# A streaming-encoder block: VectorE's sums of weight blocks in one sequence, gate multiplications later, a gate block's joins and second heads sooner, other first loads

## The chip, the cores and the metric

One core of one Trainium2 chip runs the whole program. The metric is the device time of one execution in microseconds, as the median of the timed runs.

## The reference

The input x has 256 tokens of width 2048, in float32, as all weights have. One layer is computed; every matrix product is in float32 accuracy.

```python
x = x + 0.5 * swiglu(rms_norm(x, ffn1_norm), w_gate, w_up, w_down)      # hidden width 5632
h = rms_norm(x, mix_norm)
u, q, k, v, g, a_lr = split(h @ w_in)      # pool part | linear attention with 4 heads, gate g
x = x + concat([pool_mixer(u), gla_mixer(q, k, v, g, a_lr)]) @ w_out
x = x + mem_cross_attention(rms_norm(x, xattn_norm), rms_norm(mem, mem_norm), w_q, w_kv, w_o)
x = x + 0.5 * swiglu(rms_norm(x, ffn2_norm), w_gate2, w_up2, w_down2)
out = rms_norm(x, final_norm)

def swiglu(h, w_gate, w_up, w_down):
    return (silu(h @ w_gate) * (h @ w_up)) @ w_down
```

In the mixer, the linear attention's output of each head is normalised (a factor per token and head), scaled, and multiplied by silu(g).

## The kernel before

**Units.** All weights are read once, in units of 1 MB (a tile of 128 x 2048 float32 called `raw`). A unit is loaded by SyncE into one of three `raw` tiles, split, and multiplied. The split makes two tiles of it: ScalarE casts the block to fp32r (`wh`, line 239) and VectorE subtracts that from the block (`wl`, line 240, "the low part"). A product in float32 accuracy is then three matmuls, activations-high by `wh`, activations-high by `wl`, activations-low by `wh`. `wh` and `wl` have three buffers each, so a unit can be split while the two before it are multiplied. The activations stand in `xs` (and `ys`) as a high and a low half, made by ScalarE and VectorE (lines 216 and 217).

**The stream.** `Stream` holds the list of units and of other operations (`st.op(f, after)`: `f` is traced once `after` more units have been listed). `emit` traces unit u's matmuls after the splits of units up to u + 2 (u + 1 for the first four), and a unit's load after the split of the unit three before it. Before the split of unit n, `prepare` of unit n + 1 is traced.

**Order on an engine.** The tracing order gives priorities; a scheduler then orders the instructions of each engine by its own estimate of when their inputs are there, so that what is traced later may be issued sooner. Some orders are forced: `in_turn(engine, f)` queues `f`'s instruction behind the last one so recorded on that engine (`latest`), and `behind_weights(f)` queues what `f` traces behind the last recorded ones of VectorE and ScalarE. The splits of the weights are traced with `in_turn`. A tile pool gives its buffers out again once they have been read; the tile `j` (a work space) has one buffer, and serves the squares for the row norms (line 255) and the sums of activations (`Sums.make`, lines 370 to 382).

**The feed-forward blocks.** The hidden width is cut into parts of 4, 4 and 3 blocks of 512 columns. For pairs of blocks, a gate product, an up product (eight units each) and then a down product are made. In most of them some units (0, 2 and 4 of `range(8)` for gate and up) are multiplied with seven products instead of eight (`seven`, line 435), which needs sums of weight blocks (tile `T`, made by `add_weights` on VectorE in three adds, lines 397, 400 and 401; then cast and split as weights are) and sums of activations (tile `xe`, made by `Sums.make`). `T` has one buffer. `combine` and `join` (lines 491 to 505) put the partial results together. The gate result goes through Silu on ScalarE with a row factor `Rcol` (line 741); `late_up` (line 749) multiplies gate by up; it is done for the first pair of a part while the next pair's gate product runs, and `turn` (line 759) transposes the result for the down product. The first gate product is a plain one (`block_t`, line 318).

**The opening.** SyncE loads alternately weights and columns of x (`wwide`, `load_x`). TensorE transposes x (`x_chunk`, line 632), ScalarE and VectorE make `xs` of it. The squares of x give the row norms (`x_squares`, `finish_norm`, lines 261 and 192 to 204), which the first gate eviction needs as `Rcol`.

**The gate blocks of the mixer.** `block_a` (line 303) multiplies four units and then evicts two halves with `evict(p, ps)`, here `ev_g(b)`: `joined` copies one half of a PSUM tile on ScalarE (line 276) and adds the other on VectorE (line 277). Between them lie the heads of the linear attention: `scores` (line 1022), `attend` (lines 1035 and 1038), `head_norms` (line 1057), `head_scale` (spread at line 213, applied at line 1071), two heads for each b. PSUM has four tiles (`ps`), which all of these share.

Of the kernel before, what the change touches and what calls it, by code (L numbers as in the profile page):

```python
# [92 lines left out]
def build(ctx, tc, I, out):  # L93
# [177 lines left out]
        R = rows["R"] = scope["pool"].tile([P, S], F32, tag="R", name=uid("R"))  # L271
        nc.vector.tensor_copy(R, ps[:, 0, :S])

    def joined(ps, dst, scale=None):
        c = ctile()
        nc.scalar.copy(c, ps[:, :, S:])
        nc.vector.tensor_tensor(out=dst, in0=ps[:, :, :S], in1=c, op=ALU.add)  # L277
        if scale is not None:
            nc.vector.tensor_tensor(out=dst, in0=dst, in1=bc(scale), op=ALU.mult)

# [112 lines left out]
    def add_weights(u, raw):  # L393
        t = scope["pool"].tile([P, 4 * NB], F32, tag="T", name=f"T{u}")
        w = raw.rearrange("p (b n) -> p b n", n=NB)
        v = t.rearrange("p (b n) -> p b n", n=NB)
        nc.vector.tensor_tensor(  # L397
            out=v[:, 0:2], in0=w[:, 1:3], in1=w[:, 0:1].to_broadcast([P, 2, NB]), op=ALU.add
        )
        nc.vector.tensor_tensor(out=v[:, 2], in0=v[:, 0], in1=w[:, 2], op=ALU.add)  # L400
        nc.vector.tensor_tensor(out=v[:, 3], in0=v[:, 2], in1=w[:, 3], op=ALU.add)  # L401
        return t

    def split_seven(u, raw, t):
# [149 lines left out]
    def wwide(w, n0, k0=0, nk=KT):  # L554

        def src(k):
            def load(raw):
                raw = raw.rearrange("p (k n) -> p k n", n=2 * NB)
                if len(loaded) < 3:
                    for kk in range(2):  # L560
                        parts = (0, NB) if not loaded else (0,)
                        for c in parts:
                            n = 2 * NB // len(parts)
                            wload(raw[:, kk : kk + 1, c : c + n], w, k + kk, 1, n0 + c, n)
                            next(first_loads, None)
                else:
                    wload(raw, w, k, 2, n0, 2 * NB)
                loaded.append(1)
            return load
        return [src(k0 + k) for k in range(0, nk, 2)]  # L570
# [154 lines left out]
    def ffn(wg, wu, wd, down):  # L725
# [36 lines left out]
            split(ys[:, k : k + 4, 0, :], ys[:, k : k + 4, 1, :], v)  # L762

        for i, g in enumerate(PAIRS):
            st.op(lambda g=g: x_sums.make(g), 5 + i)
        for lo, n in FF_PARTS:
            whole = n == KT // 4
            for b in range(0, n - 1, 2):
                n0 = (lo + b) * NB
                if lo == b == 0:  # L770
                    block_t(wwide(wg, n0), xs, lambda j, ps: ev_gate(j, ps, 1))
                else:
                    block_s(wwide(wg, n0), xs, x_sums, range(8), lambda j, c: ev_gate(j, c, 0))
                held, up = {}, {}
                into_down = whole and b
                block_s(wwide(wu, n0), xs, x_sums, range(8), up.__setitem__)
                st.op(lambda held=held: held.update(gate))
                for j in (1, 0):
                    st.op(lambda j=j, held=held, up=up: late_up(held, j, up[j]),
                          0 if into_down else 2)  # L780
                wait = CLEAR if b + 2 < n - 1 else 1 if into_down else 4
                for j in range(2):
                    st.op(lambda j=j, b=b, held=held: turn(held[j], 4 * (b + j)), wait)
            if n % 2:
                def both(j, ps):
                    if j:
                        ev_up(0, ps)
                    else:
                        ev_gate(j, ps, 1)
                block_t(wtwo(wg, wu, (lo + n - 1) * NB), xs, both)  # L790
                st.op(lambda n=n: turn(gate[0], 4 * (n - 1)), 1)
            if whole:
                for g, after in zip(Y_PAIRS, (2, 4)):
                    st.op(lambda g=g: behind_weights(lambda: y_sums.make(g)), after)
            down(wd, 4 * lo, 4 * n, lo + n == FF // NB, y_sums if whole else None)
# [277 lines left out]
    def ev_g(b):  # L1073
        def evict(p, ps):
            h = 2 * b + p
            t = ttile()
            joined(ps, t, rows["R"])
            nc.scalar.activation(t, t, AF.Silu)
            for vt in range(2):
                nc.vector.scalar_tensor_tensor(  # L1080
                    out=t[:, vt, :], in0=mix["oz", b][:, 2 * p + vt, :], scalar=gcol(G_HN + 2 * h + vt),
                    in1=t[:, vt, :], op0=ALU.mult, op1=ALU.mult,
                )
            split_pair(ys, 8 + 2 * h, t)
        return evict

    for b in range(2):
        block_b(wblock(w_in, (4 + b) * NB), xs, ev_v(b))
        for i in range(2):
# [2 lines left out]
            st.op(lambda h=h: scores(h), at)  # L1092
            st.op(lambda h=h: attend(h), at + 1)
            st.op(lambda h=h: head_squares(h), at + 1)
        st.op(lambda b=b: head_norms(b), 4)
        st.op(lambda b=b: head_scale(b), 5)
    block_a(wblock(w_in, 6 * NB), xs, ev_g(0))
    block_a(wblock(w_in, 7 * NB), xs, ev_g(1))
    st.op(close_scope, 1)
    st.op(open_scope("s_x"), 1)  # L1100
# [275 lines left out]
    def split_unit(u, own):  # L1376
# [11 lines left out]
        step = {0: NB, 1: 2 * NB, 2: 2 * NB}.get(u, 4 * NB)  # L1388
        for c in range(0, 4 * NB, step):
            part = slice(c, c + step)  # L1390
            split_weights(hi[:, part], lo[:, part], raw[:, part])
        return (hi, lo), None

# [38 lines left out]
```

## Time and profile before

| | us |
|---|---|
| median of 3 runs | 2137.97 (2135.68 to 2138.45) |
| profiled execution | 2137.34 |
| its span, first to last instruction | 2135.5 |
| TensorE busy (matmuls) | 2110.5, 99% of the span |
| VectorE busy | 1528.0, 72% |
| ScalarE busy | 1036.1, 49% |
| mean granted TensorE clock | 0.997 |

The profile calls the engines PE (TensorE, matmuls), PEld (TensorE, weight loads), DVE (VectorE), ACT (ScalarE), POOL (GpSimd) and SP (SyncE, which issues the loads). "pt<-wh,xs" is an instruction that writes tile pt and reads wh and xs; L240 is line 240 of the kernel. "A <- B: 2.6, 1, 1.3" in the waits says that A waited for B for 2.6 us in total, how many times, and the longest. In the chain of waits a row has start, length and what ran then. PEclk is the share of full speed that TensorE's clock was granted.

### The profile page before, as it was taken

What the parts mean: (1) busy time and instruction counts of PE and PEld (TensorE: products, weight loads), DVE (VectorE), ACT (ScalarE), POOL (GpSimd) and SP (SyncE); (2) the same over time, 40 slices, a digit from 0 to 9 for tenths busy, and PEclk for the clock granted to TensorE, in tenths of its full rate; (3) what the DMA queues carried; (4) which work ended last, traced back from release to release, by engine and by line L of the source; (5) the groups of instructions that cost most, each with busy time, mean ns of one, the idle gap of its engine ahead of it and who ended that gap; (6) DMA issues with size and microseconds to landing.
All of it is one profiled execution on the core that took longest, in us unless ns stands there. A gap on an engine that the chain in (4) does not pass through costs nothing.

```text
span 2135.5 us, 24222 instructions
## 1 busy us (share of the span) xinstructions
PE 2110.5 (99%) x10008; PEld 1764.6 (83%) x10008; DVE 1528.0 (72%) x1332; ACT 1036.1 (49%) x928; POOL 14.0 (1%) x40
## 2 busy tenths in 40 slices
PE   9999999999999999999999999999999999999998
PEld 7778888788888888878888888888888887888886
DVE  7888888888865677565656545467888878888744
ACT  7544444544543545446445444455444455444434
POOL 0000000000000000000000000000000000000001
PEclk9999999999999999999999999999999999999999
DMA  7556665566666655458655455665577655676663
GB/s 277 197 177 217 238 215 192 182 218 237 215 214 220 218 180 178 158 169 297 224 178 178 158 166 170 197 210 198 183 236 230 224 180 192 219 237 217 234 217 118
DMA packets 143606, 435.93 MB, mean 204 GB/s; under 512 B 9860, under 2 KB 13544, under 8 KB 143112
## 3 DMA queue, kind: packets, MB, share of 16 engines
q1 hardware_dynamic: 143464, 434.38, 60.4%
q8 instruction: 78, 1.28, 0.2%
q14 instruction: 32, 0.26, 0.0%
q10 hardware_dynamic: 32, 0.01, 0.0%
HBM read 417.58 MB, written 16.78 MB: 203 GB/s over the span
## 4 chain that ended last, share of the span: by engine, by line
PE 94%; DVE 3%; ACT 1%; issue 1%; DMA 0%; SPq 0%; DVEq 0%; ACTq 0%
PE pt L318 53%; PE pa L303 15%; PE pt L435 13%; PE pb L318 6%; PE pe L318 3%; DVE wl L240 1%; PE ph L759 1%; ACT wh L239 1%; DVE xl L240 1%; PE pl L1166 1%; PE pv L1201 1%; PE px L688 0%; DVE T L397 0%; PE pp L886 0%; DVE sg L749 0%
## 5 line engine op out<-in xcount | busy, mean ns | idle before, releaser
L240 DVE TENSOR_TENSOR wl<-raw,wh 128x2048 fp32r<-128x2048 f32 (+2 forms) x316 | 712.3, 2256 | 399.3 <-ACT wh L239 398.8
L239 ACT CAST wh<-raw 128x2048 fp32r<-128x2048 f32 (+2 forms) x316 | 594.9, 1884 | 561.3 <-PE pt L318 338.0
L318 PE MATMUL pt<-wh,xs 128*128 128x512 f32 x1952 | 620.8, 390 | 3.0 <-ACT wh L239 1.7
L318 PE MATMUL pt<-wh,ys 128*128 128x512 f32 x1536 | 477.4, 390 | 0.0
L318 PEld LDWEIGHTS pt<-wh,xs 128*128 128x128 f32 x1952 | 366.3, 188 | 79.6 <-ACT wh L239 2.6
L318 PE MATMUL pt<-wl,xs 128*128 128x512 f32 x976 | 380.5, 390 | 0.0
L318 PEld LDWEIGHTS pt<-wh,ys 128*128 128x128 f32 x1536 | 288.0, 188 | 59.6
L303 PE MATMUL pa<-xs,wh 128*128 128x512 f32 x896 | 317.9, 399 | 3.1 <-DVE t L277 2.6
L318 PE MATMUL pt<-wl,ys 128*128 128x512 f32 x768 | 298.9, 389 | 0.0
L303 PE MATMUL pa<-xs,wl 128*128 128x256 f32 x896 | 248.9, 281 | 0.0
L239 ACT CAST wh<-T 128x2048 fp32r<-128x2048 f32 x66 | 126.2, 1912 | 246.9 <-DVE T L401 218.7
L240 DVE TENSOR_TENSOR wl<-T,wh 128x2048 fp32r<-128x2048 f32 x66 | 151.2, 2290 | 94.0 <-ACT wh L239 94.0
L318 PEld LDWEIGHTS pt<-wl,xs 128*128 128x128 f32 x976 | 183.2, 188 | 38.2 <-DVE wl L240 0.3
L303 PEld LDWEIGHTS pa<-xs,wh 128*128 128x128 f32 x896 | 168.3, 189 | 42.5 <-issue 3.3
L303 PEld LDWEIGHTS pa<-xs,wl 128*128 128x128 f32 x896 | 169.7, 190 | 1.5
L318 PEld LDWEIGHTS pt<-wl,ys 128*128 128x128 f32 x768 | 144.2, 188 | 29.6
L318 PE MATMUL pb<-wh,xs 128*128 128x512 f32 x384 | 121.5, 392 | 0.0
L240 DVE TENSOR_TENSOR xl<-raw,xh 128x1536 fp32r<-128x1536 f32 x66 | 115.5, 1750 | 1.2 <-ACT xh L239 1.2
L435 PE MATMUL pt<-wh,xe 128*128 128x512 f32 x324 | 109.9, 393 | 2.6 <-ACT wh L239 2.6
L239 ACT CAST xh<-raw 128x1536 fp32r<-128x1536 f32 x66 | 97.6, 1478 | 15.1 <-PE pt L435 7.9
L318 PEld LDWEIGHTS pb<-wh,xs 128*128 128x128 f32 x384 | 72.1, 188 | 15.0 <-issue 0.2
L435 PE MATMUL pt<-xh,xs 128*128 128x512 f32 x216 | 80.6, 390 | 3.2 <-DVE sg L505 2.1
(231 smaller groups left out, 1919.9 us busy)
## 6 DMA issues: line engine op xcount, KB each, us to landing
raw<-in_ffn_w_down SPq DMA_DIRECT2D x88, 1024.0 KB, 5.6
raw<-in_ffn_w_up SPq DMA_DIRECT2D x80, 1024.0 KB, 5.0
raw<-in_ffn_w_gate SPq DMA_DIRECT2D x77, 1024.0 KB, 5.0
raw<-in_w_in SPq DMA_DIRECT2D x32, 1024.0 KB, 5.2
raw<-in_xattn_w_kv SPq DMA_DIRECT2D x32, 1024.0 KB, 5.2
raw<-in_w_out SPq DMA_DIRECT2D x16, 1024.0 KB, 6.3
raw<-in_xattn_w_q SPq DMA_DIRECT2D x16, 1024.0 KB, 5.1
raw<-in_xattn_w_o SPq DMA_DIRECT2D x16, 1024.0 KB, 5.6
```

The costliest lines, as they stand in the source:

```text
L239: in_turn("scalar", lambda: nc.scalar.copy(hi, src))
L240: in_turn("vector", lambda: nc.vector.tensor_tensor(out=lo, in0=src, in1=f32(hi), op=ALU.subtract))
L303: nc.tensor.matmul(o, w, x, start=k == 0 and i == 0, stop=last and i == 1)
L318: nc.tensor.matmul(ps, a, w, start=first and i == 0, stop=last and i == 2)
L435: nc.tensor.matmul(banks[n], x, w, start=n in fresh and j == 0, stop=n in ends and j == 2)
L759: nc.tensor.transpose(v[:, i, h * P : (h + 1) * P], g[:, h, i * P : (i + 1) * P], ident)
L1166: nc.tensor.matmul(ps[:, t, :M], ys[:, 4 * h + d, a, tok], xa["K"][:, d, b, :], start=i == 0, stop=i == 11,)
L1201: nc.tensor.matmul(ps[:, d, :S], xa["V"][:, m, a, col], xa["PT"][:, m, b, :], start=i == 0, stop=i == 5,)
```

## The change

1. *Sums in one sequence.* The three adds of `add_weights` are traced with `in_turn("vector", ...)`. Since `prepare` of unit n + 1 is traced ahead of the split of unit n, they are queued on VectorE behind the low part of unit n - 1 and ahead of that of unit n, with no low part between them.
2. *Gate multiplications later.* `late_up` of a part's first pair, where another pair follows, is traced three units after the up product instead of two.
3. *Sums of activations.* `Sums.make` for gate and up is traced after 4, 5 and 6 units instead of 5, 6 and 7, and queued behind the weights' split. This puts the first two of them ahead of the squares in the tracing order.
4. *The gate block.* For the first gate block both evictions are traced right after its last unit (before, the second one unit later), and the adds of its joins are recorded as `latest`, so that later low parts are queued behind them. `head_norms` and `head_scale` of the first heads come one unit later, `head_norms` of the second heads one unit sooner.
5. *First loads.* The first columns of x follow two weight pieces instead of one. In the first unit, the casts after the first quarter are queued behind the high halves of the first `xs`.

```diff
-    def joined(ps, dst, scale=None):
+    def joined(ps, dst, scale=None, first=False):
         c = ctile()
         nc.scalar.copy(c, ps[:, :, S:])
-        nc.vector.tensor_tensor(out=dst, in0=ps[:, :, :S], in1=c, op=ALU.add)
+        add = nc.vector.tensor_tensor(out=dst, in0=ps[:, :, :S], in1=c, op=ALU.add)
+        if first:
+            latest["vector"] = add
...
     def add_weights(u, raw):
...
-        nc.vector.tensor_tensor(
-            out=v[:, 0:2], in0=w[:, 1:3], in1=w[:, 0:1].to_broadcast([P, 2, NB]), op=ALU.add
-        )
-        nc.vector.tensor_tensor(out=v[:, 2], in0=v[:, 0], in1=w[:, 2], op=ALU.add)
-        nc.vector.tensor_tensor(out=v[:, 3], in0=v[:, 2], in1=w[:, 3], op=ALU.add)
+        for o, a, b in (
+            (v[:, 0:2], w[:, 1:3], w[:, 0:1].to_broadcast([P, 2, NB])),
+            (v[:, 2], v[:, 0], w[:, 2]),
+            (v[:, 3], v[:, 2], w[:, 3]),
+        ):
+            in_turn("vector", lambda: nc.vector.tensor_tensor(out=o, in0=a, in1=b, op=ALU.add))
...
                             wload(raw[:, kk : kk + 1, c : c + n], w, k + kk, 1, n0 + c, n)
-                            next(first_loads, None)
+                            if c or loaded:
+                                next(first_loads, None)
+                    if len(loaded) == 2:
+                        next(first_loads, None)
...
         for i, g in enumerate(PAIRS):
-            st.op(lambda g=g: x_sums.make(g), 5 + i)
+            st.op(lambda g=g: behind_weights(lambda: x_sums.make(g)), 4 + i)
...
                     st.op(lambda j=j, held=held, up=up: late_up(held, j, up[j]),
-                          0 if into_down else 2)
+                          0 if into_down else 3 if b + 2 < n - 1 else 2)
...
-            joined(ps, t, rows["R"])
+            joined(ps, t, rows["R"], b == 0)
...
-        st.op(lambda b=b: head_norms(b), 4)
-        st.op(lambda b=b: head_scale(b), 5)
-    block_a(wblock(w_in, 6 * NB), xs, ev_g(0))
+        st.op(lambda b=b: head_norms(b), 5 - 2 * b)
+        st.op(lambda b=b: head_scale(b), 6 - b)
+    block_a(wblock(w_in, 6 * NB), xs, ev_g(0), (0, 0))
...
         for c in range(0, 4 * NB, step):
             part = slice(c, c + step)
+            if u == 0 and c == step:
+                latest["scalar"] = rows["hi", 0]
             split_weights(hi[:, part], lo[:, part], raw[:, part])
```

## The prediction

> **What bounds the kernel now.** I read the page first, then the waits of TensorE, then the chain of waits in the stretches around each wait, last the timeline of single engines there.
>
> ```profile
> span 2135.5 us, 24222 instructions
> PE 2110.5 (99%) x10008; PEld 1764.6 (83%) x10008; DVE 1528.0 (72%) x1332; ACT 1036.1 (49%) x928; POOL 14.0 (1%) x40
> ```
>
> TensorE is busy for all but 25 us of the span, and the change takes no matmul away. So it can win only idle time of TensorE, and time in which TensorE runs slowly. The profiled execution took 2137.34 us (1.8 us lie outside the span); the median of the three timed runs is 2137.97, 0.6 more. I make the sum as a difference and take it from the median. About 0.2% (4.3 us) is what a measurement of this kernel can tell from no change.
>
> The waits of TensorE (us in total, times, longest) name nearly all of the idle time that other engines cause:
>
> ```profile
> PE pa L303 <- DVE t L277: 2.6, 1, 2.6
> PE pt L435 <- ACT wh L239: 2.6, 2, 1.3
> PE pt L435 <- DVE sg L505: 2.1, 2, 1.7
> PE pt L318 <- ACT wh L239: 1.7, 2, 0.8
> ...
> PE pt L318 <- ACT xs L216: 1.4, 1, 1.4
> PE pt L435 <- ACT sg L741: 1.1, 1, 1.1
> PE pt L435 <- DVE xl L240: 0.8, 1, 0.8
> ...
> PE po L1035 <- DVE ST L1028: 0.6, 1, 0.6
> ```
>
> That is 12.9 us in some ten places, each up to 2.6 us long, where VectorE or ScalarE came late. The edits can be set against them one by one.
>
> **Sums in one sequence, gate multiplications later.** The second and fourth rows are one place that occurs twice, in FFN 1 and at the same step of FFN 2. The chain of waits there (start, us, what):
>
> ```profile
> 367.76 2.29 DVE wl L240
> 370.05 2.65 DVE sg L749 x4
> 372.70 1.13 DVE T L397
> 373.83 1.67 DVE xl L240
> ...
> 376.94 0.06 ACT wh L239
> ```
>
> VectorE does four gate multiplications (L749), then the first block sum (L397), a low part (xl) and the other two sums; only then can ScalarE cast the sums (wh), for which TensorE waits. The change takes both things out of the way: the multiplications of a first pair of hidden blocks come one unit later, behind the next sums and low parts, which takes 2.65 us off the front; and xl may no longer stand between the sums, another 1.67. The two waits in a row at one place are (2.6 + 1.7) / 2 = 2.1 us, so 4.3 us off covers it. What is late next is the landing of the raw block, or the low part that the sums now go ahead of: that is the slower rival below. The moved multiplications still stand well before the transposes that read them, six units on, and hold up plain low parts only.
>
> After this wait, and after the 2.6 us one at 914 us, TensorE also ran slowly (columns: stretch; sum of PE, PEld, DVE, ACT, POOL busy; PEclk; DMA):
>
> ```profile
> 381.00:383.00 2.00, 1.99 (x6) 1.42 (x6) 2.00 (x2) 1.44 (x1) 0.00 (x0) 0.63 0.10 41
> 383.00:385.00 2.00, 2.00 (x7) 1.55 (x6) 2.00 (x2) 0.59 (x1) 0.00 (x0) 0.52 0.35 55
> 914.00:916.00 2.00, 1.81 (x5) 1.59 (x6) 2.00 (x5) 0.00 (x0) 0.00 (x0) 0.50 0.74 152
> 916.00:918.00 2.00, 2.00 (x9) 1.73 (x8) 1.90 (x5) 1.43 (x3) 0.00 (x0) 0.65 0.88 356
> ```
>
> The granted clock falls to a half. Over 4 us the mean was (0.63 + 0.52) / 2 = 0.58 and (0.50 + 0.65) / 2 = 0.58, so each place lost 4 x 0.42 = 1.7 us more. I count this as won with the wait. [...] The trace shows the drop after idle times of 2.6 us and less, so I go by the trace.
>
> FFN 1 gives 2.1 + 1.7 and FFN 2, whose clock stayed whole, 2.1: 5.9 us at most. I take 5.0; the ends are 5.9 and nothing.
>
> A third place, in the next block, waits first for a low part (the 0.8 us row, xl) and then for a join (L505, 2.1 - 1.7 = 0.4 us) that stands behind it. The sums' sequence changes what lies there but gives the join no right of way: I take half, 0.6 us, between 1.2 and nothing. The longer join wait (1.7 us), elsewhere, I leave as it is.
>
> **The gate block.** The longest wait stands where the first gate block ends, in the chain of waits:
>
> ```profile
> 911.02 2.30 DVE wl L240
> 913.33 0.02 issue
> 913.35 0.70 DVE t L277
> ```
>
> and ScalarE's half of the join was long done:
>
> ```profile
> 907.41 0.59 ACT L276 COPY c<-pa 128x512 f32<-128x512 f32 x1 [2.59 <-PE pa L303]
> ```
>
> The join add (t L277) could have run at 908.0; it stood behind a later block's low part (wl) and came at 913.35. The next gate block needs the PSUM tile that the add reads. In the changed kernel both joins of this block are traced at its end and the next low part is queued behind their adds, so the add comes 5.3 us sooner, twice what TensorE waited. The reordered heads help too: the second heads' products no longer take their PSUM tile behind the first heads' scaling, so the 0.6 us wait (po L1035), which falls in the same gap, moves into the block before. Behind the adds waits one low part, for a unit two units away: 2 x 0.7 us, covered. I take 2.6 + 0.6 + 1.7 of clock = 4.9 us; ends 5.3 and nothing.
>
> **The start.** TensorE, then ScalarE:
>
> ```profile
> 4.39 2.00 PE L632 MATMUL px<-ident,x 128*128 128x128 f32 x8
> 7.75 0.50 PE L318 MATMUL pt<-wh,xs 128*128 128x512 f32 x1 [1.36 <-ACT xs L216]
> ```
>
> ```profile
> 6.70 0.62 ACT L239 CAST wh<-raw 128x512 fp32r<-128x512 f32 x1 [1.30 <-DMA raw<-in_ffn_w_gate]
> 7.22 0.83 ACT L216 ACTIVATE xs<-px,gains 128x256 fp32r<-128x256 f32 x2
> ```
>
> The activations (xs) stand behind the second quarter's cast, which waited for its DMA. The change queues that cast behind them and loads the weight pieces before the x columns. The 1.4 us wait should nearly go: a lead of 1.1 us.
>
> It will not last. The lead runs on to the first up block, where TensorE waits for the first gate eviction (sg L741, the 1.1 us row), and that for the row factors:
>
> ```profile
> L255 ACT ACTIVATE j<-x x16: 406/418/428, 15.3 to 46.4; 128x256 f32<-128x256 f32 x16
> L255 ACT ACTIVATION_READ_ACCUMULATOR j<-x x16: 185/190/211, 15.6 to 46.7; 128x1 f32 x16
> L370 DVE TENSOR_TENSOR j<-xs x3: 670/681/683, 10.6 to 60.8; 128x512 f32<-128x512 f32 x3
> ```
>
> ```profile
> 33.78 2.29 DVE L240 TENSOR_TENSOR wl<-raw,wh 128x2048 fp32r<-128x2048 f32 x1 [1.64 <-ACT wh L239]
> ...
> 48.82 0.16 DVE L261 TENSOR_REDUCE sums<-ss 128x2 f32<-128x16 f32 x1
> ...
> 60.74 0.15 DVE L204 RECIPROCAL Rcol<-chain 128x2 f32<-128x2 f32 x1
> ```
>
> From reduction to factor it takes 12 us, small VectorE steps with big ones between them. The squares (L255) and the activations' sums (L370) share one tile, j. Before, the first sums went ahead of the squares and the second waited for the last of them. In the changed kernel two sums are traced ahead of the squares, the second behind the low part that here ran 33.78 to 36.07. If j goes round in the order of the trace, no square can run before about 38 us (36.1, the add of 0.68, four smaller steps and the split), and 16 squares at 0.42 with a read-out of 0.19 each, which overlap a little, are some 9 us: they end at 47 to 50 instead of 47. Against that, one set of sums less lies in VectorE's way afterwards. Bounds for start and opening together: 2 us better (the lead and the 1.1 us wait for sg) to 3 worse (squares 3 us later). I take nothing.
>
> **New small waits.** Each of the 66 sums now goes ahead of the low part of the unit before it. One sequence costs (timeline of VectorE)
>
> ```profile
> 484.41 1.22 DVE L397 TENSOR_TENSOR T<-raw 128x1024 f32<-128x1024 f32 x1
> 485.66 0.69 DVE L400 TENSOR_TENSOR T<-T,raw 128x512 f32<-128x512 f32 x1
> 486.39 0.69 DVE L401 TENSOR_TENSOR T<-T,raw 128x512 f32<-128x512 f32 x1
> ```
>
> 2.7 us, and at this place it already stands ahead of the next low part, and the waits above hold none of this place. I put 1.5 us for waits elsewhere, between 0 and the 13 us of the slower rival below.
>
> **Sum:** 5.0 + 0.6 + 4.9 + 0 - 1.5 = 9.0 us off 2137.97: 2129.0.
>
> **The rivals.** *Low parts come late (slower).* Place: units before a block sum in the tight gate and up blocks. VectorE and TensorE there:
>
> ```profile
> 415.80 2.29 DVE L240 TENSOR_TENSOR wl<-raw,wh 128x2048 fp32r<-128x2048 f32 x1
> ...
> 420.42 0.39 PE L318 MATMUL pt<-wl,xs 128*128 128x512 f32 x1
> ```
>
> The low part is ready at 418.09, 2.3 us before TensorE uses it; pushed back by a 2.7 us sequence it is 0.4 us late. If the sums then also wait for a raw block, the low part waits with them. It decides from the point where VectorE does not win back as much by earlier casts. If about 35 of the 66 (where the sums now follow that low part) lost 0.4 us, that is 14 us instead of my 1.5: about 2142. Against it: VectorE is busy only 72%, and in these blocks it sat idle waiting for the cast of the sums, which the new order fills.
>
> *The row factors come later.* The opening loses the 3 us by which the squares may end later, and a wait that long may drop the clock for 1.7 us as at 914 us: 2132 to 2133.7. For it stands the shared tile; against it, that fewer steps lie between reduction and factor.
>
> *The waits only move.* A scheduler orders each engine's queue, and the added edges change its whole order; TensorE's queue too is interleaved from several units. Waits may come back at other places, as large: about 2138.
>
> **How the numbers follow.** Forecast 0.62 (its own range 2123 to 2134), late low parts 0.16, late row factors 0.10, waits that move 0.12. Faster by over 0.2% (below 2133.7): 0.60 from the forecast, 0.07 from late row factors, 0.01 from moved waits: 0.68. Within 0.2%: 0.02 + 0.03 + 0.09 = 0.14. Slower: 0.16 + 0.02 = 0.18. The range 2123 to 2140 takes in the best end of the start, the late row factors, the moved waits and the mild part of the late low parts.
>
> **What would show it.** In the profile after, the waits of TensorE should have no row for t L277 and none for wh L239 under L435 beyond 1 us; PEclk should be whole around 380 and 910 us; L749 should come behind a wl from T; L397, L400 and L401 should follow each other 66 times with 0.04 us between; the first L318 matmul should start near 6.5 us. If a row "PE pt <- DVE wl L240" of several us with many times appears, the slower rival is right; if "PE pt L435 <- ACT sg L741" grows, the row factors are late. I am wrong if the waits sum to 12 us or more again.

## The result, and the profile after

The changed kernel takes 2131.97 us (2129.47 to 2133.83, 7 runs) where the kernel before takes 2138.23 (2135.43 to 2140.49): a ratio of 0.9971, with a 95% interval of 0.996 to 0.9983. That is 6.3 us faster; 9.0 were forecast. The profiled execution of the changed kernel took 2133.83 us, its slowest, so that the two traces differ by 3.5 us of span only.

The page of the changed kernel, its span and the busy time of each engine:

```profile
span 2132.0 us, 24229 instructions
PE 2109.4 (99%) x10008; PEld 1766.1 (83%) x10008; DVE 1530.9 (72%) x1332; ACT 1043.3 (49%) x928; POOL 12.9 (1%) x40
```

The work is the same. The waits of TensorE, of which this is all that the view has (us in total, times, longest; the lines have moved by 3 to 7, so that L439 is L435 of before, L321 is L318, L748 is L741):

```profile
PE pt L439 <- ACT sg L748: 6.9, 1, 6.9
PE px L639 <- DMA x<-in_x: 2.8, 1, 2.8
PE pwarm L186 <- POOL ident masks.py:199: 1.4, 1, 1.4
PE pt L439 <- DVE wl L240: 1.4, 1, 1.4
PE pa L306 <- DVE xs L217: 0.4, 1, 0.4
```

Every wait that the prediction quoted from the middle of the kernel is gone: the block sums' casts, the low part xl, both joins, the gate block's add. Two new ones of 6.9 and 2.8 us stand in the first 75 us. So the change won in the body and paid at the opening.

**The body.** Groups of instructions (busy, mean ns | idle of the engine before them, and what ended it). Before:

```profile
L239 ACT CAST wh<-T 128x2048 fp32r<-128x2048 f32 x66 | 126.2, 1912 | 246.9 <-DVE T L401 218.7 <-PE pt L318 21.3 <-issue 6.6
L240 DVE TENSOR_TENSOR wl<-T,wh 128x2048 fp32r<-128x2048 f32 x66 | 151.2, 2290 | 94.0 <-ACT wh L239 94.0
```

After:

```profile
L239 ACT CAST wh<-T 128x2048 fp32r<-128x2048 f32 x66 | 126.4, 1915 | 116.5 <-PE pt L321 75.5 <-DVE T L405 27.0 <-issue 13.6
L240 DVE TENSOR_TENSOR wl<-T,wh 128x2048 fp32r<-128x2048 f32 x66 | 151.0, 2287 | 22.7 <-ACT wh L239 22.7
L405 DVE TENSOR_TENSOR T<-raw 128x1024 f32<-128x1024 f32 x66 | 80.7, 1223 | 23.7 <-DMA raw<-in_ffn_w_gate 12.4 <-DMA raw<-in_ffn_w_up 10.1 <-DMA raw<-in_ffn_w_down 0.6
```

ScalarE waited 218.7 us for finished block sums, now 27.0; VectorE in turn waited 94.0 us for the cast of the sums, now 22.7. The sums themselves now wait 23.7 us for landing blocks, and none of that reaches TensorE. At the place in FFN 1 where the first of the forecast waits stood, VectorE's timeline after reads:

```profile
370.56 2.28 DVE L240 TENSOR_TENSOR wl<-T,wh 128x2048 fp32r<-128x2048 f32 x1
372.88 1.23 DVE L405 TENSOR_TENSOR T<-raw 128x1024 f32<-128x1024 f32 x1
374.14 1.42 DVE L405 TENSOR_TENSOR T<-T,raw 128x512 f32<-128x512 f32 x2
...
382.01 2.73 DVE L756 SCALAR_TENSOR_TENSOR sg<-sg,Rcol,sg 128x512 f32<-128x512 f32 x4
```

The three adds run one behind the other, and the multiplications (L756, before L749) come behind the next low part from T. Both stretches with a slow clock are whole (stretch; sum of PE, PEld, DVE, ACT, POOL busy; PEclk; DMA share; GB/s). The third row is the new slow one:

```profile
69.00:76.00 7.00, 3.79 (x10) 3.00 (x11) 0.86 (x2) 5.11 (x7) 0.00 (x0) 0.52 0.00 0
377.00:381.00 4.00, 4.00 (x19) 3.31 (x18) 3.62 (x3) 2.34 (x2) 0.00 (x0) 1.00 0.52 152
905.00:915.00 10.00, 10.00 (x61) 8.90 (x61) 5.35 (x8) 2.93 (x3) 0.00 (x0) 1.00 0.50 143
```

**Where the 3.5 us come together.** The start of one and the same matmul in both traces, first down product, first logits, last down product. Before:

```profile
185.28 0.39 PE L318 MATMUL pt<-wh,ys 128*128 128x512 f32 x1
...
1160.35 0.28 PE L1166 MATMUL pl<-K,ys 128*128 128x256 f32 x1
...
2059.58 0.39 PE L318 MATMUL pe<-wh,ys 128*128 128x512 f32 x1
```

After:

```profile
195.26 0.39 PE L321 MATMUL pt<-wh,ys 128*128 128x512 f32 x1
...
1159.92 0.28 PE L1173 MATMUL pl<-K,ys 128*128 128x256 f32 x1
...
2056.10 0.39 PE L321 MATMUL pe<-wh,ys 128*128 128x512 f32 x1
```

At 195 us the changed kernel is 10.0 us behind, although the join wait at 141 us (1.85 us between the two matmuls beyond their usual distance) has gone: the opening costs 11.8. The rest of FFN 1 gives back 6.1, the gate block 4.8, FFN 2 3.0; some 0.4 is lost again between these.

**The opening.** First the start, TensorE after:

```profile
4.38 1.11 PE L639 MATMUL px<-ident,x 128*128 128x128 f32 x4
8.32 1.12 PE L639 MATMUL px<-ident,x 128*128 128x128 f32 x4 [2.82 <-DMA x<-in_x]
9.08 0.78 PE L321 MATMUL pt<-wh,xs 128*128 128x512 f32 x1
```

The first matmul of the product starts at 9.08, not 7.75. It is not the cast or xs that it waits for: the transposes of the second columns of x stand ahead of it in TensorE's queue (as they did before, at 4.39), and those columns' load is now issued behind a second weight piece, at 2.19 instead of 1.73, and lands at 8.27 instead of 5.43. A landing this late does not come with the order each time: e1, e2 and e12 below issue the same loads in the same order, and there TensorE waits 1.3, 0.8 and 1.1 us for it instead of 2.8, while with the loads as before it waits 1.0 us or less in ten traces. Until about 14.3 us the matmuls then follow at 0.42 us, before at 0.23. Next, the squares (duration in ns min/median/max, first and last start):

```profile
L255 ACT ACTIVATE j<-x x16: 408/418/421, 56.0 to 65.8; 128x256 f32<-128x256 f32 x16
```

They ran from 15.3 to 46.4 before. They wait for tile j, which the first two sums of activations now hold, the second last; VectorE's timeline shows how long (j, and xe made from it):

```profile
42.19 0.68 DVE L373 TENSOR_TENSOR j<-xs 128x512 f32<-128x512 f32 x1
...
43.39 0.29 DVE L380 TENSOR_TENSOR j<-j 128x128 f32<-128x128 f32 x1
...
46.40 0.29 DVE L381 TENSOR_TENSOR j<-j 128x128 f32<-128x128 f32 x1
...
48.66 0.28 DVE L382 SCALAR_TENSOR_TENSOR j<-j 128x128 f32<-128x128 f32 x1
...
51.52 0.29 DVE L385 TENSOR_TENSOR j<-j 128x128 f32<-128x128 f32 x1
...
53.25 0.69 DVE L246 TENSOR_TENSOR xe<-j,xe 128x512 fp32r<-128x512 f32 x1
...
66.93 0.16 DVE L261 TENSOR_REDUCE sums<-ss 128x2 f32<-128x16 f32 x1
69.03 0.17 DVE L204 RECIPROCAL Rcol<-chain 128x2 f32<-128x2 f32 x1
```

Six steps of 2.5 us together take 11.7 us, since a low part or a block sum lies between any two of them. After two casts of ScalarE the squares start at 56.0; with another cast between them they end at 66.3, the factor comes at 69.2 instead of 60.9, and TensorE waits 6.9 us for the first gate eviction. On ScalarE the eviction comes 1.7 us behind the factor: the cast of the third sums and a table load for the eviction's line stand between. Before, both were done while the eviction waited for the factor. ScalarE, before:

```profile
57.22 1.28 ACT L741 ACT_TABLE_LOAD   x1
60.93 1.27 ACT L741 ACTIVATE sg<-pt,Rcol 128x512 f32<-128x512 f32 x2 [2.42 <-DVE Rcol L204]
```

After:

```profile
69.59 1.28 ACT L748 ACT_TABLE_LOAD   x1
70.89 1.27 ACT L748 ACTIVATE sg<-pt,Rcol 128x512 f32<-128x512 f32 x2
```

### The profile page after: what moved, and what is told of

The parts are those of the page before. It is cut to its first block, busy times and chain, and to the rows that moved or that the text cites. A ratio compares the mean times of both kernels' runs of the same rounds, so it can differ in the third digit from the quotient of the medians.

```text
span 2132.0 us, 24229 instructions
## 1 busy us (share of the span) xinstructions
PE 2109.4 (99%) x10008; PEld 1766.1 (83%) x10008; DVE 1530.9 (72%) x1332; ACT 1043.3 (49%) x928; POOL 12.9 (1%) x40
## 3 DMA queue, kind: packets, MB, share of 16 engines
q8 instruction: 78, 1.28, 0.2%
## 4 chain that ended last, share of the span: by engine, by line
PE 98%; ACT 1%; DVE 0%; DMA 0%; issue 0%; SPq 0%; DVEq 0%; ACTq 0%
PE pt L321 56%; PE pa L306 15%; PE pt L439 15%; PE pb L321 6%; PE pe L321 3%; PE ph L766 1%; PE pl L1173 1%; PE pv L1208 1%; PE px L695 0%; ACT j L255 0%; DMA x<-in_x 0%; PE pp L893 0%; ACT wh L239 0%; PE px L639 0%; PE pa L920 0%; PE po L1042 0%
## 5 line engine op out<-in xcount | busy, mean ns | idle before, releaser
L321 PE MATMUL pt<-wh,xs 128*128 128x512 f32 x1952 | 618.4, 391 | 0.0
L321 PE MATMUL pt<-wh,ys 128*128 128x512 f32 x1536 | 477.2, 390 | 0.0
L321 PEld LDWEIGHTS pt<-wh,xs 128*128 128x128 f32 x1952 | 367.3, 188 | 75.9
L321 PE MATMUL pt<-wl,xs 128*128 128x512 f32 x976 | 380.8, 390 | 0.0
L321 PEld LDWEIGHTS pt<-wh,ys 128*128 128x128 f32 x1536 | 288.0, 188 | 59.4
L321 PE MATMUL pt<-wl,ys 128*128 128x512 f32 x768 | 299.0, 389 | 0.0
L321 PEld LDWEIGHTS pt<-wl,xs 128*128 128x128 f32 x976 | 183.8, 188 | 38.2 <-DVE wl L240 0.2
L306 PEld LDWEIGHTS pa<-xs,wh 128*128 128x128 f32 x896 | 167.7, 188 | 39.7 <-DVE xs L217 0.8
L321 PEld LDWEIGHTS pt<-wl,ys 128*128 128x128 f32 x768 | 144.2, 188 | 29.8
L240 DVE TENSOR_TENSOR wl<-T,wh 128x2048 fp32r<-128x2048 f32 x66 | 151.0, 2287 | 22.7 <-ACT wh L239 22.7
L321 PE MATMUL pb<-wh,xs 128*128 128x512 f32 x384 | 121.6, 392 | 0.0
L439 PE MATMUL pt<-wh,xe 128*128 128x512 f32 x324 | 111.0, 390 | 0.0
L405 DVE TENSOR_TENSOR T<-raw 128x1024 f32<-128x1024 f32 x66 | 80.7, 1223 | 23.7 <-DMA raw<-in_ffn_w_gate 12.4
L405 DVE TENSOR_TENSOR T<-T,raw 128x512 f32<-128x512 f32 x132 | 90.9, 689 | 2.7
```

What stands on the lines that cost most here:

```text
L240: in_turn("vector", lambda: nc.vector.tensor_tensor(out=lo, in0=src, in1=f32(hi), op=ALU.subtract))
L306: nc.tensor.matmul(o, w, x, start=k == 0 and i == 0, stop=last and i == 1)
L321: nc.tensor.matmul(ps, a, w, start=first and i == 0, stop=last and i == 2)
L405: in_turn("vector", lambda: nc.vector.tensor_tensor(out=o, in0=a, in1=b, op=ALU.add))
L439: nc.tensor.matmul(banks[n], x, w, start=n in fresh and j == 0, stop=n in ends and j == 2)
```

## The experiments

Kernels with the same time in the column "before" share the runs of the kernel before; kernels of different groups are compared by their ratios. "Factor" is when the last step of the row factors ends (L204), "gate wait" the wait of TensorE for the first gate eviction (sg).

| kernel | us | before | ratio, 95% | factor at | gate wait |
|---|---|---|---|---|---|
| after | 2131.97 | 2138.23 | 0.9971 (0.996 to 0.9983) | 69.2 | 6.9 |
| e1 sums of activations as before | 2123.46 | 2139.15 | 0.9927 (0.9915 to 0.994) | 61.8 | 1.1 |
| e2 squares in a tile of their own | 2126.88 | 2139.15 | 0.9945 (0.9933 to 0.9958) | 62.2 | 3.0 |
| e3 loads as before | 2130.86 | 2139.15 | 0.9962 (0.995 to 0.9975) | 65.3 | 7.1 |
| e7 e1 and e3 together | 2120.14 | 2139.15 | 0.9911 (0.9898 to 0.9925) | 50.6 | none |
| e4 gate block alone | 2134.17 | 2138.43 | 0.998 (0.9971 to 0.9989) | 63.7 | 1.1 |
| e5 later multiplications alone | 2137.41 | 2138.43 | 0.9996 (0.9987 to 1.0005) | 61.1 | 1.1 |
| e6 sums in sequence alone | 2129.87 | 2138.43 | 0.9966 (0.9954 to 0.9979) | 62.3 | 1.1 |
| e8 e7 without the cast's place | 2124.88 | 2138.43 | 0.9941 (0.9929 to 0.9954) | 63.2 | 1.1 |
| e9 e2 and e3 together | 2120.81 | 2137.57 | 0.9918 (0.9905 to 0.9932) | 51.4 | none |
| e10 e7 with multiplications as before | 2121.74 | 2137.57 | 0.9927 (0.9915 to 0.994) | 50.5 | none |
| e11 e7 with the second columns later | 2124.32 | 2137.57 | 0.9939 (0.9925 to 0.9952) | 61.2 | 1.1 |
| e12 sums early, not queued | 2124.12 | 2137.57 | 0.9936 (0.9924 to 0.9949) | 61.6 | 1.3 |

The theory: the loss lies in the opening alone, and there in the sums of activations (part 3 of the change), which hold the squares' tile; the new loads cost a smaller part. The rivals: the loads are the main loss; or the squares come late for another reason, VectorE's or ScalarE's order.

### Which edit of the opening costs what

**e1**, from the changed kernel:

```diff
-            st.op(lambda g=g: behind_weights(lambda: x_sums.make(g)), 4 + i)
+            st.op(lambda g=g: x_sums.make(g), 5 + i)
```

> The changed kernel, with the sums of activations traced and ordered as before (after 5, 6 and 7 units, not behind the weights); all else of the change stays. Theory (the squares wait for the tile j, which the second sums now hold first): the row factors come some 8 us sooner than in the changed kernel, the 6.9 us wait of TensorE for the gate eviction shrinks to under 2.5 us, and the time falls by about 8 us, ratio to before 0.993. Rival (the block sums in one sequence push the norm's small steps back on VectorE): the wait stays within 2 us of 6.9 and the ratio stays 0.997.

0.44% less than after by the ratios, 9.4 us. The waits of TensorE in e1 have

```profile
PE pt L439 <- ACT sg L748: 1.1, 1, 1.1
```

The gate wait is what it was before the change, and the mean clock of the profiled execution is 0.999 (0.997 in after). The theory holds, and with its size. In the trace the first matmul is sooner as well, at 7.52 with the same loads, by the earlier landing named above.

**e2**, from the changed kernel: the sums of activations stay where the change put them, the squares get another tile (in bfloat16, for room; the squares are written there and not read, only their sums are).

```diff
-            j = tmp.tile([P, S], F32, tag="j", name=uid("j"))
+            j = tmp.tile([P, S], mybir.dt.bfloat16, tag="q", name=uid("q"))
```

> The changed kernel, with one edit: the squares write their (unused) products to a tile of their own, in bfloat16 so that it fits; the row sums stay float32. The sums of activations stay early and behind the weights. Theory (shared tile): squares run again from about 16 us on, the factors are there near 60 us, the ratio falls to about 0.993 as in the run with the sums as before. Rival (it is the place of the sums on VectorE, not the tile): the squares move but the wait stays above 5 us, ratio 0.997.

0.26% less than after, 5.6 us: the shared tile is most of what e1 takes back. The squares run from 9.7 to 47.1 and the reduction at 48.8, as before the change. It stays short of the expectation, although the factor comes at 62.2, nearly as in e1 (61.8). The third sums are still early and queued: their cast ends only at 62.16 on ScalarE, the table load of 1.28 us follows it, and the eviction starts at 63.47. In e1 cast and table load are done by 59.4, and the eviction starts at 61.81, with the factor. The gate wait of 3.0 us is followed by a stretch at half clock (same columns as above):

```profile
64.00:70.80 6.80, 6.01 (x14) 4.76 (x15) 1.11 (x1) 3.79 (x5) 0.00 (x0) 0.50 0.00 0
```

6.0 us of work at half speed are 3.0 us lost.

**e3**, from the changed kernel:

```diff
-                            if c or loaded:
-                                next(first_loads, None)
-                    if len(loaded) == 2:
-                        next(first_loads, None)
+                            next(first_loads, None)
```

> The changed kernel, with the first loads in the order of before (x columns and weight pieces in turn from the start); the cast's place in the first unit stays. Theory (the transposes of the second x columns stand ahead of the first matmul on TensorE, so their late landing delays it by 2.8 us and leaves the clock at a half until 14 us): the first matmul comes at 6.5 to 7 us instead of 9.1, clock whole from about 6 us, the start gains 4 us; since the row factors still come late, 2 to 4 us of that reach the end, ratio 0.9955. Rival (the opening ends at the row factors, whatever the start): ratio 0.997, the wait for the gate eviction grows by what the start gained.

The first matmul starts at 6.59 us, 2.5 sooner, and the wait for x falls to 0.3 us. When the clock became whole there, expected at about 6 us, is not shown here. By the ratios 1.9 us are left at the end (0.9962 and 0.9971), but the intervals overlap, and theory and rival cannot be told apart by them. In the trace the gate wait is about as long, 7.1 us, and not longer by what the start gained, as the rival had it; the first down product starts at 192.62, 2.6 us sooner: the factor moves with the start (65.3 instead of 69.2), and a longer drop of the clock takes back a part (mean 0.53 from 64 to 75 us, which is some 10.3 us at half; 6.8 in after).

**e7**, both edits together:

> The changed kernel with both the sums of activations and the first loads as before. Theory: the opening's whole loss goes, 11 to 12 us of the changed kernel's time by the profiles: about 2122, ratio 0.992. Rival (the two losses hide one another, so that taking both away gives no more than the larger): 2124, as with the sums alone.

This is the lowest ratio of all, 19.0 us below the kernel before, and 0.9911 against 0.9971 for the change as it was made. e1 was timed in the same rounds, and each of its times (2123.1 to 2124.0) lies above each of e7's (2118.9 to 2121.4): with the sums as before, the loads cost 3.3 us by the medians. Its waits, but for the constant 1.4 us at the very start and 0.4 for xs:

```profile
PE pt L321 <- DVE wl L240: 0.9, 1, 0.9
PE pt L439 <- DVE sg L509: 0.8, 2, 0.7
```

No gate wait is left at all; the kernel before had one of 1.1 us, so this opening is shorter than that one too (first down product at 180.69 instead of 185.28, 1.85 of it by the join wait that is gone). From reduction to factor it takes 6.2 us, 12.1 in the kernel before (VectorE):

```profile
44.45 0.16 DVE L261 TENSOR_REDUCE sums<-ss 128x2 f32<-128x16 f32 x1
...
45.25 2.29 DVE L240 TENSOR_TENSOR wl<-T,wh 128x2048 fp32r<-128x2048 f32 x1
47.46 0.16 DVE L196 RECIPROCAL Rcol<-chain 128x2 f32<-128x2 f32 x1
...
50.46 0.16 DVE L204 RECIPROCAL Rcol<-chain 128x2 f32<-128x2 f32 x1
```

Only one low part and one set of block sums lie within the chain. In e2 one set, two adds of a second and three low parts do, and it takes 13.4 us; in e1, e4, e5, e6, e8, e9, e11 and e12 it takes 11.6 to 12.1.

**e12**, from the changed kernel: as early in the tracing as the change has it, without the queueing.

```diff
-            st.op(lambda g=g: behind_weights(lambda: x_sums.make(g)), 4 + i)
+            st.op(lambda g=g: x_sums.make(g), 4 + i)
```

> The changed kernel with the sums of activations traced early as in it (after 4, 5 and 6 units) but not queued behind the weights. Theory (the squares wait for j because the second sums, which come first in it, are queued behind the seventh unit's low part): without the queue the sums go as soon as their activations are there, the squares follow from about 20 us on, the wait for the gate eviction is 3 us or less: 2123 to 2127, ratio 0.993 to 0.9945. Rival (the early place in the tracing order alone is what does it): as the changed kernel, ratio 0.997.

0.35% less than after, 7.5 us, near e1, as the theory had it. The scheduler is then free to run the second sums early (the first sums' add starts at 9.96 us, the second's at 19.29, the third's at 48.92), and the squares run from 27.4 to 47.3. So not the place in the tracing does the damage, but that the sums are tied behind low parts that run at 37 to 40 us while a later user of the same tile is tied behind the sums.

**e9**, e2's tile and e3's loads, the sums queued as the change has them:

> The changed kernel with both repairs that keep its early sums: the squares on a tile of their own (bfloat16, unused products) and the first loads as before. Theory: the squares no longer wait, but as with the own tile alone the norm's small steps still take some 13 us from reduction to factor, with a wait of 3 us and a slow clock at the gate eviction; the start gives 1 to 3 us: 2124 to 2126, ratio 0.9935 to 0.9945. Rival (with an early start the small steps find gaps as in the kernel with sums and loads as before): 2120, ratio 0.991.

The rival was right and the theory not: with the early start the reduction comes at 39.7, so even a chain of 11.6 us ends at 51.4, ahead of need. e9 and e7 cannot be told apart.

### The cast's place and the start

**e8**, from e7:

```diff
-            if u == 0 and c == step:
-                latest["scalar"] = rows["hi", 0]
```

> The changed kernel with sums of activations and first loads as before, and also without the queueing of the first unit's casts behind the first activations. Theory: the first matmul comes at 7.75 us again instead of 6.26, and since the row factors are no longer late there, the 1.5 us reach the end: ratio 0.9918 beside 0.9911 of the same kernel with the queueing. Rival (the factors still end the opening): no difference, 0.9911.

Against its own kernel before it has 0.9941, e7 0.9911: some 6 us more, where the theory gave this edit the 1.2 to 1.5 us of the start and the rival nothing: both missed. The first matmul comes at 7.50 instead of 6.26; but the whole opening takes another order as well, with the factor at 63.2 instead of 50.6 and the 1.1 us gate wait back. In the traces its first down product starts 5.3 us later than e7's (185.97 against 180.69), which is nearly all of the difference between the two spans (5.5).

**e11**, from e7: the second columns of x are transposed one unit later, so that they do not stand ahead of the first matmul.

```diff
-        st.op(lambda c=c: x_chunk(c), c - 1 if c < 3 else c - 2)
+        st.op(lambda c=c: x_chunk(c), 1 if c < 3 else c - 2)
```

> The changed kernel with sums of activations and first loads as before, and the transposes of the second x columns traced one unit later, so that they stand behind the first matmuls on TensorE. Theory: the first matmul no longer waits for a second load; with these loads that wait is small, so 0 to 1 us off, ratio 0.9906 to 0.9911. Rival (the second columns come late for unit 1, or the other order of the opening brings back the late factors): slower by over 1 us, ratio above 0.9916.

The first matmul comes 0.2 us sooner, at 6.06, and the kernel is slower (0.9939): again the factor comes at 61 us. The rival was right.

### The body

Each of these is the kernel before with one part of the change. **e4**, the gate block alone:

```diff
+        if first:
+            latest["vector"] = add
...
-            joined(ps, t, rows["R"])
+            joined(ps, t, rows["R"], b == 0)
...
-        st.op(lambda b=b: head_norms(b), 4)
-        st.op(lambda b=b: head_scale(b), 5)
-    block_a(wblock(w_in, 6 * NB), xs, ev_g(0))
+        st.op(lambda b=b: head_norms(b), 5 - 2 * b)
+        st.op(lambda b=b: head_scale(b), 6 - b)
+    block_a(wblock(w_in, 6 * NB), xs, ev_g(0), (0, 0))
```

> The kernel before with the gate-block part of the change alone. Theory: the wait for the join (2.6 us), the one for the scores (0.6) and the slow clock behind them (1.7) go, nothing else moves: 4.9 us off, ratio 0.9977. Rival (the wait moves to the heads, whose products now stand closer together): less than 2.5 us off, ratio above 0.9988, with a new wait between 880 and 915 us.

4.3 us by the medians, and 4.8 between the same two matmuls in the traces. The waits t L277 and po L1035 are gone. As expected.

**e5**, the later multiplications alone:

```diff
-                          0 if into_down else 2)
+                          0 if into_down else 3 if b + 2 < n - 1 else 2)
```

> The kernel before with the gate multiplications one unit later, alone. Theory (the four multiplications, 2.65 us, stood ahead of the sums, and that is more than the 2.1 us wait): both waits for wh at the third sum of that block go, with the slow clock in FFN 1, 5.9 us off, ratio 0.9972; the waits at 141 and 405 us stay. Rival (the low part xl between the sums is what makes them late): about 2 us off, ratio 0.999.

No difference, by the interval. VectorE, then TensorE, at the place in FFN 1:

```profile
376.73 2.73 DVE L749 SCALAR_TENSOR_TENSOR sg<-sg,Rcol,sg 128x512 f32<-128x512 f32 x4
379.38 6.69 DVE L240 TENSOR_TENSOR wl<-raw,wh 128x2048 fp32r<-128x2048 f32 x3
```

```profile
381.72 0.50 PE L318 MATMUL pt<-wl,xs 128*128 128x512 f32 x1 [2.29 <-DVE wl L240]
```

The multiplications leave the front of the sums and stand in front of a low part that TensorE needs as soon: a wait of 2.3 us takes the place of one of 1.3 and one of 0.8. The rival's size was near, its mechanism (the cast still waits) was not what happened. The prediction had counted the low parts that the moved multiplications hold up as free. Against the expectation the join wait at 141 us is gone here too; those at 405 us stay.

**e6**, the sums in one sequence alone:

```diff
-        nc.vector.tensor_tensor(out=v[:, 2], in0=v[:, 0], in1=w[:, 2], op=ALU.add)
...
+        for o, a, b in (
...
+            in_turn("vector", lambda: nc.vector.tensor_tensor(out=o, in0=a, in1=b, op=ALU.add))
```

> The kernel before with the block sums in one sequence with the low parts, alone. Theory (the sequence is traced ahead of the low part behind which the multiplications stand, so it passes them as well): the two waits for wh go too, and the waits at 141 and 405 us with them, since VectorE no longer idles for the casts of the sums: 5.9 + 1.8 + 1.5 = 9 us off, ratio 0.9957. Rival (slower: low parts come late behind the sums): new waits for wl, at most 3 us off, ratio above 0.9985.

7.3 us by the ratio (9 were expected), with the multiplications where they were: no less than the 6.3 us of the whole change. All the waits of the feed-forward blocks are gone, at 141 and 405 us too. VectorE:

```profile
361.65 1.22 DVE L402 TENSOR_TENSOR T<-raw 128x1024 f32<-128x1024 f32 x1
362.91 1.42 DVE L402 TENSOR_TENSOR T<-T,raw 128x512 f32<-128x512 f32 x2
364.24 2.28 DVE L240 TENSOR_TENSOR wl<-raw,wh 128x2048 fp32r<-128x2048 f32 x1
366.44 2.73 DVE L750 SCALAR_TENSOR_TENSOR sg<-sg,Rcol,sg 128x512 f32<-128x512 f32 x4
```

The sums pass the multiplications by themselves. The slower rival, low parts that come late, did not appear: the only wait of TensorE for a low part in this kernel is the 0.7 us one of the opening, which the kernel before has as well.

**e10**, from e7, asks whether the later multiplications add anything to the sums:

```diff
-                          0 if into_down else 3 if b + 2 < n - 1 else 2)
+                          0 if into_down else 2)
```

> The changed kernel with sums of activations and first loads as before, and the gate multiplications traced after two units as before too. Theory (the sums in sequence pass the multiplications already, since these are queued behind the low part that follows the sums): no difference from the same kernel with the later multiplications, ratio 0.9911. Rival (the multiplications still hold a low part or a cast up): 2 us or more slower, ratio above 0.992.

0.9927 against 0.9911, with intervals that overlap. A join wait of 1.0 us and one of 0.7 for ys stand in its trace where e7 has 0.7 and 0.9 elsewhere. The spans are 0.3 us apart (2119.9 and 2119.6). Not told apart: 3.4 us by the ratios, where the rival would be right, nothing by the traces.

## Why the prediction was right or wrong

**Sums and multiplications (5.0 forecast): too small, and wrong about who earns it.** The two wh waits went with the clock loss in FFN 1. Between the same matmuls they give 4.6 us in FFN 1 (the 6.1 less 1.5 at 405 us) and 3.0 in FFN 2, 7.6 together, above the 5.9 that the prediction held for the most: the way between the matmuls of a place is longer than its rows of waits (3.0 against 2.1 in FFN 2). But the prediction gave 2.65 us of the way to the later multiplications and 1.67 to the sums' sequence. Alone, the first brought nothing (e5) and the second everything (e6), since a queue that ties the sums to the low part before them also carries them past the multiplications.

**The third place (0.6) and the join wait left as it is (0).** Both went whole: 1.5 us at 405 and 1.85 at 141. The prediction said that the new order "gives the join no right of way". In the changed kernel it needs none. That the joins come up sooner because VectorE no longer idles for the cast of the sums fits the rows above, but was not tested by itself: the wait at 141 went in e5 too, with the sums as before, and join waits of 0.2 to 1.2 us come back in e1, e7, e8, e10, e11 and e12.

**New small waits (1.5 worse): none.** Earlier casts paid for the later low parts, which was the condition that the prediction named for its rival.

**The gate block (4.9): right**, 4.8 in the trace of after and of e4, with 4.3 by e4's medians. Its 1.7 us of clock is the less certain part, since a drop of this kind comes in some executions and not in others (below); with this wait in place it came in the two traces for which the clock there is shown (0.50 from 913.99 to 917.40 us in before, 0.51 from 909.80 to 913.30 in e6).

**Start and opening (0, between 2 better and 3 worse): the step that failed.** It measured 11.8 us worse in the profiled execution. By the times it is less: that execution was the slowest of seven, the two traces differ by 3.5 us and the medians by 6.3, which leaves an estimate of 9 us for the opening if the body gave the same 15.3. (e7 is some 13 us below the changed kernel by the ratios, but its opening is shorter than that of the kernel before.) Three things in it were mis-sized.

- "The 1.4 us wait should nearly go: a lead of 1.1 us." The wait for xs went, and one for the x columns came: 1.3 us later instead of 1.1 sooner. The part of the change that loads a weight piece before the second x columns was costed without asking what stands ahead of the first matmul in TensorE's own queue. The wait that the prediction went by was itself ended by xs, which the transposes feed.
- "No square can run before about 38 us" was a bound from below that was then taken for the time. The prediction placed the second add behind the low part of 33.8, and counted its steps end to end (0.68 and four of 0.3). In the trace that low part is the one at 37.5 (the start's loss), the add runs at 42.2, and its steps take 11.7 us, since they have no right of way between low parts. The prediction had this very pattern before it, in the factor chain that takes 12 us for less than 1 us of work, and did not apply it to the steps of the sums.
- The factor was put at up to 3 us late. It came 8.3 us late (69.2 against 60.9), and the eviction another 1.7 behind it, by the cast and the table load. TensorE waited 6.9 instead of 1.1 us, and then had half clock from 68.9 to 75.7, of which it worked 3.5 us: 1.8 more, which the sum left out and only the rival had.

Put together for the profiled execution: 1.3 for the later first matmul, 2.6 for 5.2 us of half clock at the start, 0.7 for the longer wait for wl, 5.8 for the gate wait, and 1.8 for the clock make 12.2, against 11.8 measured between the matmuls. The first two are in part that execution's: in e1, e2 and e12, with the same loads, the first matmul starts at 7.1 to 7.6, and the clock at the start is not the same in each execution (below). The rival "the row factors come later" was right in kind, but priced at 3 to 4.7 us, where the gate wait and its clock loss cost 7.6. That the total came near the forecast is luck, and owes to two errors of opposite sign: the opening 12 worse, the body 6 better (15.3 instead of 9).

**The signs that the prediction named.** Those of the body came: no row for t L277 or wh, a whole clock around 380 and 910 us, the multiplications behind a low part from T. Those of the opening did not: the first matmul starts at 9.08, not 6.5, low parts and other steps stand between the sums there, and the row for sg L741 grew to 6.9 us, which the prediction had named as the sign of late factors. All rows of waits sum to 12.9 us (15.4 before), over the 12 by which it called itself wrong; without the rows of 1.4 (pwarm) and 0.4 us (pa), which both kernels have, it is 11.1.

Left open: why the scheduler's order brings the factor at 50 to 51 us in e7, e9 and e10 and at 61 to 64 in all others whose squares are not held up. One small edit moves the whole opening from one order to the other (e8, e11), and the reduction comes sooner in the first three (40 to 44 against 49 to 52 us). That was seen and not taken apart.

## What to carry to other kernels

When a small job is queued behind something large, list what else uses its buffers: here a work space with one buffer passed the delay on to the row norms, and through them to TensorE. A chain of short steps on an engine that carries long ones can take the long ones' time: from reduction to factor there are five steps from one to the next, and they took 12.1 us in the kernel before, 6.2 in e7 and 2.3 in the changed kernel, by what lay between them. Count what can come between such steps, not their durations. And the forced order that was worth most here is the one that stopped an engine from idling for its own consumer (the sums, 7.3 us): it also cleared waits that were never its target.

## What the runs showed of the hardware

**Short waits halve the clock in some executions and not in others.** In e4 the feed-forward waits are those of the kernel before. In the kernel before the clock fell after the wait in FFN 1 (0.50 from 381.51 to 384.92 us) and stayed whole in FFN 2 (1.00 from 1777.56 to 1784.39); in e4 it is the other way round:

```profile
381.00:385.00 4.00, 2.35 (x8) 1.42 (x9) 3.23 (x2) 4.00 (x3) 0.00 (x0) 1.00 0.70 249
1778.40:1781.80 3.40, 2.95 (x7) 2.24 (x8) 3.40 (x3) 2.19 (x2) 0.00 (x0) 0.50 0.29 120
```

The drops last 3.4 us in the kernel before, in e4 (above) and at the gate block of e6 (0.51 from 909.80 to 913.30), at waits of 2.1 to 2.6 us; the same once more near 9 us in e6 (0.98 from 0 to 9 us and 0.71 from 9 to 14.3), at a wait of 1.5; 6.8 in e2 (0.50 from 64.0 to 70.8, at 3.0 us) and in the changed kernel (0.50 from 68.89 to 75.72, at 6.9); and some 10.3 in e3 (0.53 from 64 to 75), at 7.1. In the trace of the kernel before the changes of the clock come at 6.04, 381.51, 384.92, 913.99, 917.40 and 2129.13 us, which is 110, 1, 155, 1 and 355 times 3.413 us apart; in that of the changed kernel at 14.28, 68.89, 75.72 and 2127.13 us, 16, 2 and 601 times.

The length of a wait alone does not tell: both places of the kernel before have waits of 1.28 and 0.84 us. In FFN 1 TensorE worked 1.76 of the 3.41 us before the drop (378.10 to 381.51). In FFN 2, counted on from the drops by whole multiples of 3.413 us, the two waits fall on two stretches, in which it worked 2.13 us (1777.56 to 1780.97) and 2.56 us (1780.97 to 1784.39). Before the drop at 913.99 us it worked 0.99 of 3.41 us, and before the one at 68.89 us in the changed kernel none. That the work within such a stretch decides fits these places; it was not tested by itself.

**The clock at the start is a matter of the execution too.** With the same first part of the program, TensorE ran at full spacing from the first product on in the kernel before (0.23 us from one matmul to the next), and in e4 only from 13.7 us (16 instructions in the 2.3 us from there). The windows from 8 to 13.7 us, before and then e4, hold 30 and 13 instructions:

```profile
8.00:13.70 5.70, 5.70 (x30) 4.76 (x30) 5.22 (x13) 3.69 (x8) 0.00 (x0) 1.00 1.03 385
```

```profile
8.00:13.70 5.70, 5.63 (x13) 4.47 (x14) 5.21 (x13) 3.73 (x8) 0.00 (x0) 1.00 1.02 383
```

PEclk reads 1.00 in both, as it does in the changed kernel from 9.0 to 14.2 us, where the matmuls follow at 0.42 us: the record of the clock begins only at 6.04 us in the trace of before and at 14.28 in that of after; here it is the spacing that tells. e4's row factors come 2.8 us later (63.7 instead of 60.9), and 5.63 us of work at about half speed make 2.8 (an estimate from the window). So part of the 2.6 us that the profiled execution of after lost there is chance, and 2 us between two traces of this kernel need not be the kernels' difference.
